# Seven places instead of four for split weight pieces in the first of two fused transformer blocks

## Chip, cores and metric

The program runs on one NeuronCore of a Trainium2 chip. The metric is the device time of one execution in microseconds (us). Before the change three runs gave 1586.46, 1587.95 and 1588.61 us; their median, 1587.95 us, is the time before. The core holds five engines that work side by side: PE (matmul), DVE and POOL (element-wise), ACT (activation, copies) and SP, which here only starts transfers from HBM.

## What is computed

Two blocks follow one another on 256 tokens of width 1024, all in fp32. The first has two layers; each is a mix of three attentions and then an MLP with a hidden width of 4096. The second block is a mixer (latent attention and an mLSTM) and a mixture of 16 experts, of which each takes 32 tokens.

```python
def hybrid_layer(x, mem, pos, g_mix, w_in, w_pa, w_pb, w_pm, w_o, g_mem, w_mkv, g_mlp, w_up, w_down):
    h = rms_norm(x, g_mix)
    z = h @ w_in
    ...
    x = x + y @ w_o
    hm = rms_norm(x, g_mlp)
    x = x + jnp.square(jax.nn.relu(hm @ w_up)) @ w_down
    return x
```

The second block adds `mixer(...)` and `ec_moe(...)`: each expert computes `silu(xs @ w_gate) * (xs @ w_up) @ w_down` on the tokens that it takes, scaled by its gate.

## The kernel before

**A weight's way to PE.** `load_w` (L311) loads a tile of weights of 1 MB, `wr`, in one transfer on SP's queue; there are four such buffers (`WR`). `pieces` (L328) cuts the tile into four pieces of 128 x 512 and splits each into two parts, since PE takes a rounded fp32 format here: ACT casts the piece into its high part (L346), and DVE (L352), or POOL for a set share of the pieces (L350), subtracts that from the piece for the low part. Both go into a *place* of the tile `wh`, which holds `WH` = 4 of them, used in turn. PE multiplies a piece in 12 matmuls (`three` L355, which calls `mm` L289: high by high, high by low, low by high). A place comes free when PE has read its piece, and a `wr` buffer when its four pieces have been split. So a split can run at most four pieces ahead of PE.

**The activations' way to PE.** The residual is `xT`, in eight parts. At each hand-over from one half of a layer to the next, `split_and_sum` (L482) adds the last product to `xT` (L478, DVE), splits each part into `hx` (ACT L426, DVE L427), and squares it (ACT L489) and sums the squares on POOL (L491). `rstd_cols` makes 1/rms of the sum (matmul `ps_mlp`, DVE L462, POOL L463), `bcast_rows` spreads it (matmul `ps_bc`, DVE L472).

**The MLP.** `mlp` (L864) runs over 16 columns of 256 hidden units. `up(c)` is 48 matmuls of four pieces, and piece j needs parts 2j and 2j+1 of `hx`. `relu2` (L881, L882, L424) turns `up` into `ux`; `accumulate` multiplies it by `w_down`, 48 matmuls `dn` for each column, two columns behind (`LAG` = 2). PE's program after a hand-over is up(0), `ps_mlp`, 12 matmuls of up(1), `ps_bc`, the rest of up(1), up(2), and the first `dn`.

**Side work in the MLPs.** `mod_rows` (L924) multiplies rows of `w_modT` on DVE and sums them (the result is `macc`). In the second MLP `context` also squares and sums `ctxT` (`ssc`: ACT L447 and L450, POOL L451), scales it (`modt` L968, DVE) and splits it (`xh`: ACT L974, DVE L975), and `gate_weights` (L1083 to L1097) prepares small weights on DVE. A row of `mod_rows` is tied behind the split before it by `tc.issue_after(behind[0])`.

**Order.** PE's order is that of the program. The orders of DVE, ACT, POOL and SP come from a scheduler at build time: it places work by priority, and splits carry a raised one (`tc.high_priority(offset=HP)`). Where a place is not yet free in the scheduler's reckoning, the split comes later in the order. In the first layer's MLP the list `HMQ` = (None, None, 0, 2) ties piece 2 of up(0) behind part 0 of `hx`, and piece 3 behind part 2; the second layer's MLP has no such tie. Two pools matter: `whl` holds `wh` for the whole program, and `b1p` lies on the right side of the on-chip memory until `b1.close()` (L1582), after the second layer's MLP; behind that, expert weights (`ew`, from `load_e`, transfers at L1502) use its room.

Of the kernel before, what the change touches and what calls it, by code (L numbers as in the profile page):

```python
# [9 lines left out]
FR = mybir.dt.float32r  # L10
# [6 lines left out]
PIECE = 512  # L17
WR = 4
WH = 4
LAG = 2  # L20
TL = 20
FH = 4.0
# [212 lines left out]
def drain(gen):  # L235
    for _ in gen:
        pass
# [3 lines left out]
def fused_kernel(ctx: ExitStack, tc: tile.TileContext, I, out):  # L241
# [30 lines left out]
    b1p = b1.enter_context(tc.tile_pool(name="b1p", bufs=1, side="right"))  # L272
# [8 lines left out]
    def vc(n, j=0, w=1):  # L281
        o = vcols[n][0] + j
        return vbuf[:, o:o + w]
# [27 lines left out]
    def load_w(src, parts=1):  # L311
        K, n = src.shape[1], src.shape[2]
        t = wrp.tile([128, 2048], FT, tag="wr", name="wr")
        v = t[:, :K * n].rearrange("p (k n) -> p k n", k=K)
        for a in range(0, K, K // parts):
            nc.sync.dma_start(out=v[:, a:a + K // parts], in_=src[:, a:a + K // parts])
        return v

    share = [0.0, 0.0]
    whx = whl.tile([128, 2, WH * PIECE], FR, tag="w", name="wh")  # L320
    whi, wlo = whx[:, 0], whx[:, 1]
    np_ = [0]

    hold = []

# [2 lines left out]
    def pieces(v, small=0):  # L328

        K, n = v.shape[1], v.shape[2]  # L330
        step = max(1, PIECE // n)
        for k0 in [*range(small), *range(small, K, step)]:
            k1 = k0 + 1 if k0 < small else min(K, k0 + step)
            for n0 in range(0, n, PIECE):
                n1 = min(n, n0 + PIECE)
                src = v[:, k0:k1, n0:n1]
                p0 = np_[0] % WH * PIECE
                np_[0] += 1
                sz = (k1 - k0) * (n1 - n0)
                hv = whi[:, p0:p0 + sz].rearrange("p (k n) -> p k n", k=k1 - k0)  # L340
                lv = wlo[:, p0:p0 + sz].rearrange("p (k n) -> p k n", k=k1 - k0)
                with ExitStack() as es:
                    es.enter_context(tc.high_priority(offset=HP))
                    for ins in hold.pop(0) if hold else ():
                        es.enter_context(tc.issue_after(ins))
                    A.copy(hv, src)  # L346
                    share[1] += share[0]
                    if share[1] >= 1:
                        share[1] -= 1
                        behind[1] = G.tensor_tensor(lv, src, hv.bitcast(FT), op=OP.subtract).ins  # L350
                    else:
                        behind[0] = V.tensor_tensor(lv, src, hv.bitcast(FT), op=OP.subtract).ins  # L352
                yield k0, k1, n0, hv, lv
# [6 lines left out]
    def hi_lo(pl, K, tag, **kw):  # L360

        t = pl.tile([128, 2, K, 256], FR, tag=tag, name=tag, **kw)
        return t[:, 0], t[:, 1], t
# [37 lines left out]
    def accumulate(w, dn, x2, kx, first, last):  # L401

        def one(k, m, hv, lv, m0, kk):
            ms = slice((m - m0) * 128, (m - m0 + 1) * 128)
            three(dn[m // 2][:, (m % 2) * 256:(m % 2) * 256 + 256], hv[:, kk, ms], lv[:, kk, ms], x2[:, :, kx + k],
                  first and k == 0 and m % 2 == 0, last and k == 1)

        if last:

            for q in range(4):  # L410
                for k0, k1, _, hv, lv in pieces(w[:, :, q * 256:(q + 1) * 256]):
                    for m in (2 * q, 2 * q + 1):
                        for k in range(k0, k1):
                            one(k, m, hv, lv, 2 * q, k - k0)
        else:
            for k0, k1, n0, hv, lv in pieces(w):
                for k in range(k0, k1):
                    for m in range(n0 // 128, n0 // 128 + hv.shape[2] // 128):
                        one(k, m, hv, lv, n0 // 128, k - k0)
# [24 lines left out]
    def square_sum(xv, K, ssum, tp):  # L444
        for k in range(K):
            if k == 0:
                A.square(ssum, xv[:, 0])  # L447
            else:
                t = tp.tile([128, 256], FT, tag="sq", name="sq", bufs=2)
                A.square(t, xv[:, k])  # L450
                G.tensor_tensor(ssum, ssum, t, op=OP.add)  # L451

    def rstd_cols(ssum, n, nm, bank=None):

        ps = (bank or acc_tile)("ps_" + nm)
        halves = [ssum] if len(ssum.shape) == 2 else [ssum[:, i] for i in range(ssum.shape[1])]
        for t in range(2):
            for i, v in enumerate(halves):
                mm(ps[:, t:t + 1], v[:, t * 128:(t + 1) * 128], ones[:, 0:1], t + i == 0, i == len(halves) - 1)
        r = sm.tile([128, 2], FT, tag="rc_" + nm, name="rc_" + nm, bufs=2)  # L460
        with tc.high_priority(offset=HR):
            V.tensor_scalar(r, ps[:, 0:2], 1.0 / n, EPS, op0=OP.mult, op1=OP.add)  # L462
            G.tensor_tensor(r, r, mhalf[:, 0:2], op=OP.pow)  # L463
        return r
# [17 lines left out]
    def split_and_sum(dn, g0, tp, queue=()):  # L482
        hh, hl, hx = hi_lo(tp, 8, "hx")
        ssum = tp.tile([128, 256], FT, tag="ssum", name="ssum", bufs=2)
        parts = []
        for k in updated(dn):
            parts.append(split_x(xT[:, k], hh[:, k], hl[:, k], vc(g0[0], g0[1] + k)))
            sq = ssum if k == 0 else tp.tile([128, 256], FT, tag="sq", name="sq", bufs=2)
            A.square(sq, xT[:, k])  # L489
            if k:  # L490
                G.tensor_tensor(ssum, ssum, sq, op=OP.add)  # L491
        hold[:] = [() if k is None else parts[k] for k in queue]
        return (hh, hl, hx), ssum
# [370 lines left out]
    def mlp(l, mp, side, dn):  # L864

        urs = [mp.tile([128, 2, 256], FT, name=f"ur{i}") for i in range(2)]
        us = [hi_lo(mp, 2, f"ux{i}") for i in range(LAG + 1)]
        xs, ssum = split_and_sum(dn, ("g_mlp", l * 8), mp, () if l else HMQ)
# [8 lines left out]
        def relu2(o):  # L877
            r = urs[nu[0] % 2]
            uh, ul, ux = us[nu[0] % (LAG + 1)]
            nu[0] += 1  # L880
            V.scalar_tensor_tensor(r, pair(o), 0.0, both(rb), op0=OP.max, op1=OP.mult)  # L881
            A.square(r, r)  # L882
            split_x(r, uh, ul)
            return ux
# [6 lines left out]
        for c in range(1, 16):  # L891
# [7 lines left out]
            cur.append(relu2(o2))  # L899
            if c >= LAG:  # L900
                accumulate(load_w(I["w_down"][l, c - LAG]), dn, cur.pop(0), 0, c == LAG, False)
            for _ in range(side[1] + (l == 0 and c in MS1)):
                next(side[0], None)
        for c in range(16 - LAG, 16):
            accumulate(load_w(I["w_down"][l, c]), dn, cur.pop(0), 0, False, c == 15)
# [640 lines left out]
    with tc.tile_pool(name="mp1", bufs=1, reuse_waits="tile") as mp:  # L1546
        src = mp.tile([128, 8, 256], FT, name="ctxT")
        nc.sync.dma_start(out=src, in_=I["ctxT"])

        def context():  # L1550
            yield
            ssum = mp.tile([128, 256], FT, tag="rbc", name="ssc")
            square_sum(src, 8, ssum, mp)
            yield
            yield
            rcc = rstd_cols(ssum, 1024, "in", fl_tile)
            yield
            rbc = mp.tile([128, 256], FT, tag="rbc", name="rbc")
            bcast_rows(rcc, rbc, fl_tile)
            yield from modulated(src, rbc, sc1[:, 1], modT[:, 1, 0:8], mp, into(ch, cl))  # L1560

        def chain(*gens):
            for g in gens:
                yield from g

        def side():
            rg = mod_rows(8, 24, (0,), mp)
            cg = context()
            bg = chain(diagonals("wv4", 0), gate_weights(wg, mp), diagonals("wq4", 1))
            for n in range(40):  # L1570
                if n % 2 == 0:
                    next(cg, None)
                next(rg, None)
                next(bg, None)
                yield

        sg = side()
        dn = mlp(1, mp, (sg, 2), dn)
        drain(sg)
        V.tensor_tensor(modT[:, 0, 16:48], macc[:, 0, 16:48], vc("b_mod", 16, 32), op=OP.add)  # L1580
        V.scalar_tensor_tensor(sc1[:, 2], modT[:, 0, 32:40], 1.0, vc("n2", 0, 8), op0=OP.add, op1=OP.mult)
    b1.close()  # L1582
    xs = hh, hl, _ = hi_lo(x2p, 8, "hx")
    mlx = ctx.enter_context(ExitStack())
# [176 lines left out]
    for j in range(4):  # L1761
# [5 lines left out]
        for i in range(2):  # L1767
            k = 2 * j + i
# [205 lines left out]
    for ci, n in enumerate(LAST):  # L1974
        c0, w = i * 128, n * 128
        for _ in range(n):
            cc = (i % 4) * 128
            for kh in range(2):
                parts = expert_tile()
                kp = 4 // len(parts)  # L1980
                for k in range(4):
                    t = parts[k // kp].rearrange("p (k e c) -> p k e c", e=4, c=128)
# [45 lines left out]
```

## Time and profile before

| | |
|---|---|
| median of 3 runs | 1587.95 us (1586.46 to 1588.61) |
| the profiled execution's own time | 1588.72 us |
| its span in the trace | 1586.9 us |
| mean granted clock of PE over the span | 0.948 of full speed |
| PE, DVE, ACT, POOL busy | 1387.1, 898.2, 675.9, 232.7 us |
| first block | 0 to about 803.6 us of the span |
| experts | from about 1156 us to the end |

The span is what the trace covers; the execution's own time lies 1.8 us above it. Rows of a timeline give start, length, engine, line, operation, output <- inputs, and in brackets how long the engine was idle just before and which work ended that wait. A name such as `wh` stands for all places of that name.

### The profile page before, as it was taken

The numbers are of one execution on the slowest core, as the hardware profiler recorded it, in microseconds if no ns is written. First come the engines' busy times: TensorE is split into PE (matmuls) and PEld (weight loads), VectorE is DVE, ScalarE is ACT, GpSimd is POOL, SyncE is SP. The second block draws the span as 40 slices with busy tenths as digits, with TensorE's granted clock in tenths as the row PEclk, the third lists the DMA queues.
The fourth block names the chain that finished last, engine by engine and source line by source line (L and its number), as shares of the span: only waits on it lengthen the run. The fifth ranks groups of instructions, "written<-read, shape, count | busy, mean of one in ns | idle before, by whom it ended". The sixth has DMA issues, their size and how long they took to land. (4 is left out here: it accounts for less than half of the span.)

```text
span 1586.9 us, 27036 instructions
## 1 busy us (share of the span) xinstructions
PE 1387.1 (87%) x10903; PEld 1153.8 (73%) x10903; DVE 898.2 (57%) x1615; ACT 675.9 (43%) x1341; POOL 232.7 (15%) x204
## 2 busy tenths in 40 slices
PE   8999999999999999999988999999888665656565
PEld 7999999999999998999987889989743111111113
DVE  8876688777787578897789775885320000000001
ACT  7566555555557556555556666555310000000001
POOL 3100022121210015322144200210100000000000
PEclk9999999999999999999998999999989878787978
DMA  8544446666543456767763322374979999999997
GB/s 315 178 145 143 160 168 248 244 222 229 196 145 132 166 185 230 266 252 279 268 250 108 134 78 80 131 275 145 366 302 424 427 428 427 428 428 426 428 427 322
DMA packets 50557, 404.87 MB, mean 255 GB/s; under 512 B 5504, under 2 KB 7424, under 8 KB 14464
## 3 DMA queue, kind: packets, MB, share of 16 engines
q1 hardware_dynamic: 50288, 403.04, 65.6%
q8 instruction: 85, 1.39, 0.3%
q14 instruction: 40, 0.33, 0.1%
q10 hardware_dynamic: 144, 0.11, 0.0%
HBM read 402.08 MB, written 1.05 MB: 254 GB/s over the span
## 5 line engine op out<-in xcount | busy, mean ns | idle before, releaser
L346 ACT CAST wh<-wr 128x512 fp32r<-128x512 f32 (+1 forms) x647 | 394.1, 616 | 351.5 <-PE up L289 81.2
L352 DVE TENSOR_TENSOR wh<-wr,wh 128x512 fp32r<-128x512 f32 (+1 forms) x563 | 403.8, 727 | 154.7 <-ACT wh L346 152.5
L289 PE MATMUL up<-hx,wh 128*128 128x256 f32 x1536 | 194.5, 285 | 7.6 <-DVE wh L352 4.9
L289 PEld LDWEIGHTS up<-hx,wh 128*128 128x128 f32 x1536 | 187.7, 192 | 10.9 <-DVE wh L352 6.6
L289 PE MATMUL dn<-ux,wh 128*128 128x256 f32 x1536 | 189.7, 283 | 0.4 <-DVE wh L352 0.4
L289 PEld LDWEIGHTS dn<-ux,wh 128*128 128x128 f32 x1536 | 186.6, 192 | 1.0 <-DVE wh L352 0.8
L350 POOL TENSOR_TENSOR wh<-wr,wh 128x512 fp32r<-128x512 f32 (+1 forms) x84 | 117.6, 1400 | 463.5 <-ACT wh L346 434.1
L1946 DVE TENSOR_TENSOR ew<-up,ew 128x512 f32<-128x512 f32 x8 | 5.5, 692 | 251.4 <-PE up L289 251.4
L289 PE MATMUL gate<-hx,wh 128*128 128x256 f32 x1152 | 141.6, 284 | 0.0
L289 PEld LDWEIGHTS gate<-hx,wh 128*128 128x128 f32 x1152 | 139.1, 192 | 1.4 <-issue 1.4
L289 PE MATMUL y<-ew 128*32 128x128 f32 (+1 forms) x896 | 76.0, 488 | 42.5 <-DMA ew<-in_w_e_down_dram 41.8
L289 PE MATMUL up<-ew,xsr 128*32 128x512 f32 x384 | 65.4, 815 | 52.7 <-DMA ew<-in_w_e_up_dram 52.7
L289 PE MATMUL gate<-ew,xsr 128*32 128x512 f32 x384 | 60.9, 764 | 50.2 <-DMA ew<-in_w_e_gate_dram 50.2
L1940 ACT ACTIVATE ew<-gate 128x512 f32<-128x512 f32 x8 | 4.8, 597 | 208.6 <-PE gate L289 207.3
L289 PEld LDWEIGHTS y<-ew 128*32 128x32 f32 x896 | 28.1, 122 | 88.2 <-DMA ew<-in_w_e_down_dram 50.7
L289 PEld LDWEIGHTS up<-ew,xsr 128*32 128x32 f32 x384 | 12.4, 131 | 106.6 <-DMA ew<-in_w_e_up_dram 74.7
L289 PEld LDWEIGHTS gate<-ew,xsr 128*32 128x32 f32 x384 | 11.9, 124 | 96.5 <-DMA ew<-in_w_e_gate_dram 64.3
L289 PE MATMUL z<-hx,wh 128*128 128x256 f32 x576 | 74.1, 286 | 4.0 <-ACT wh L346 1.2
L289 PE MATMUL tanh<-hx,wh 128*128 128x256 f32 x576 | 77.0, 287 | 0.2 <-DVE wh L352 0.2
L289 PEld LDWEIGHTS z<-hx,wh 128*128 128x128 f32 x576 | 70.4, 191 | 6.8 <-DVE hx L427 1.6
L289 PEld LDWEIGHTS tanh<-hx,wh 128*128 128x128 f32 x576 | 71.5, 191 | 1.2 <-DVE wh L352 0.5
L924 DVE SCALAR_TENSOR_TENSOR wr<-wr,srow 128x1024 f32<-128x1024 f32 x48 | 68.5, 1432 | 0.0
(451 smaller groups left out, 1991.8 us busy)
## 6 DMA issues: line engine op xcount, KB each, us to landing
ew<-in_w_e_up_dram SPq DMA_DIRECT2D x26, 2048.0 KB, 22.1
ew<-in_w_e_down_dram SPq DMA_DIRECT2D x25, 2048.0 KB, 21.4
ew<-in_w_e_gate_dram SPq DMA_DIRECT2D x24, 2048.0 KB, 21.4
wr<-in_w_up_dram SPq DMA_DIRECT2D x32, 1024.0 KB, 4.9
wr<-in_w_down_dram SPq DMA_DIRECT2D x32, 1024.0 KB, 5.4
wr<-in_w_gates_dram SPq DMA_DIRECT2D x24, 1024.0 KB, 4.8
wr<-in_w_modT_dram SPq DMA_DIRECT2D x24, 1024.0 KB, 4.9
wr<-in_w_in_dram SPq DMA_DIRECT2D x24, 1024.0 KB, 4.8
```

The costliest lines, as they stand in the source:

```text
L289: PE.matmul(o, l, r, start=st, stop=sp, skip_group_check=True)
L346: A.copy(hv, src)
L350: behind[1] = G.tensor_tensor(lv, src, hv.bitcast(FT), op=OP.subtract).ins
L352: behind[0] = V.tensor_tensor(lv, src, hv.bitcast(FT), op=OP.subtract).ins
L924: V.scalar_tensor_tensor(d, w[:, j], 0.5, srow[v], op0=OP.mult, op1=OP.mult, accum_out=macc[:, v, 2 * i + j:2 * i + j + 1])
L1940: A.activation(h[:, j * 512:(j + 1) * 512], gate[j], AF.Silu)
L1946: V.tensor_tensor(h[:, c], up[j], h[:, c], op=OP.mult)
```

## The change

Three more places are allocated in the pool `b1p`, as a second tile `wx_` that is also named `wh`. A list `places` holds the seven in turn: each new piece takes the one that was used longest ago. At the end of the first block the three are struck from the list, and four are used from there on. Nothing is said of `HMQ`, of priorities or of the share of POOL.

```diff
@@ -17,6 +17,7 @@
 PIECE = 512
 WR = 4
 WH = 4
+WX = 3
 LAG = 2
 TL = 20
 FH = 4.0
@@ -318,8 +319,10 @@
 
     share = [0.0, 0.0]
     whx = whl.tile([128, 2, WH * PIECE], FR, tag="w", name="wh")
-    whi, wlo = whx[:, 0], whx[:, 1]
-    np_ = [0]
+    wx_ = b1p.tile([128, 2, WX * PIECE], FR, name="wh")
+
+    places = [(t[:, 0, a:a + PIECE], t[:, 1, a:a + PIECE], t is whx) for t, n in ((whx, WH), (wx_, WX))
+              for a in range(0, n * PIECE, PIECE)]
 
     hold = []
 
@@ -334,11 +337,9 @@
             for n0 in range(0, n, PIECE):
                 n1 = min(n, n0 + PIECE)
                 src = v[:, k0:k1, n0:n1]
-                p0 = np_[0] % WH * PIECE
-                np_[0] += 1
+                places.append(places.pop(0))
                 sz = (k1 - k0) * (n1 - n0)
-                hv = whi[:, p0:p0 + sz].rearrange("p (k n) -> p k n", k=k1 - k0)
-                lv = wlo[:, p0:p0 + sz].rearrange("p (k n) -> p k n", k=k1 - k0)
+                hv, lv = [p[:, :sz].rearrange("p (k n) -> p k n", k=k1 - k0) for p in places[-1][:2]]
                 with ExitStack() as es:
                     es.enter_context(tc.high_priority(offset=HP))
                     for ins in hold.pop(0) if hold else ():
@@ -1579,6 +1580,7 @@
         drain(sg)
         V.tensor_tensor(modT[:, 0, 16:48], macc[:, 0, 16:48], vc("b_mod", 16, 32), op=OP.add)
         V.scalar_tensor_tensor(sc1[:, 2], modT[:, 0, 32:40], 1.0, vc("n2", 0, 8), op0=OP.add, op1=OP.mult)
+    places[:] = [p for p in places if p[2]]
     b1.close()
     xs = hh, hl, _ = hi_lo(x2p, 8, "hx")
     mlx = ctx.enter_context(ExitStack())
```

PE's order does not change at all. On DVE, ACT, POOL and SP nearly all moved instructions are splits: throughout the first block, each other instruction now has three more casts ahead of it than before. SP issues two small side loads (`ctxT`, `wgt`) one place later. Behind `b1.close()` all orders agree.

In the rows below a number behind a name tells buffers apart: `wh_95` are the old places (in both versions), `wh_96` the new ones, and `wr_` names the loaded tile, whose number the change shifts by one. Line numbers of the new version lie one higher.

DVE at the hand-over to the first layer's MLP, before. `wr_2689` is up(0), `wr_2754` is up(1), `dn0` and `dn1` are the last product of the attention half:

```order
L478 TENSOR_TENSOR xT_84<-xT_84,dn0_2169 128x512 x2
L352 TENSOR_TENSOR wh_95<-wr_2689,wh_95 128x512
L478 TENSOR_TENSOR xT_84<-xT_84,dn1_2170 128x512
L427 SCALAR_TENSOR_TENSOR hx_2641<-xT_84,vbuf_83,hx_2641 128x256
L478 TENSOR_TENSOR xT_84<-xT_84,dn1_2170 128x512
L427 SCALAR_TENSOR_TENSOR hx_2641<-xT_84,vbuf_83,hx_2641 128x256 x4
L352 TENSOR_TENSOR wh_95<-wr_2689,wh_95 128x512
L427 SCALAR_TENSOR_TENSOR hx_2641<-xT_84,vbuf_83,hx_2641 128x256 x3
L352 TENSOR_TENSOR wh_95<-wr_2689,wh_95 128x512
L352 TENSOR_TENSOR wh_95<-wr_2754,wh_95 128x512 x2
L462 TENSOR_SCALAR rc_mlp_2750<-ps_mlp_2747 128x2
```

The same place with the change (`wr_2690` is up(0), `wr_2755` up(1)):

```order
L479 TENSOR_TENSOR xT_84<-xT_84,dn0_2170 128x512 x2
L353 TENSOR_TENSOR wh_96<-wr_2755,wh_96 128x512 x2
L479 TENSOR_TENSOR xT_84<-xT_84,dn1_2171 128x512 x2
L428 SCALAR_TENSOR_TENSOR hx_2642<-xT_84,vbuf_83,hx_2642 128x256 x2
L353 TENSOR_TENSOR wh_96<-wr_2755,wh_96 128x512
L428 SCALAR_TENSOR_TENSOR hx_2642<-xT_84,vbuf_83,hx_2642 128x256 x3
L353 TENSOR_TENSOR wh_95<-wr_2690,wh_95 128x512
L428 SCALAR_TENSOR_TENSOR hx_2642<-xT_84,vbuf_83,hx_2642 128x256 x3
L353 TENSOR_TENSOR wh_95<-wr_2690,wh_95 128x512
L353 TENSOR_TENSOR wh_95<-wr_2755,wh_95 128x512
L925 SCALAR_TENSOR_TENSOR modd_2832,macc_497<-wr_2830,srow_496 128x1024
L463 TENSOR_SCALAR rc_mlp_2751<-ps_mlp_2748 128x2
```

Three pieces of up(1) now stand ahead of up(0)'s pieces 2 and 3, which are still tied behind `hx`; the first `hx` stands behind both additions to `xT`; and a row of `mod_rows` stands ahead of `rc_mlp`.

ACT at the hand-over to the second layer's MLP, before. `wr_6966`, `wr_7031` and `wr_7108` are up(0), up(1) and up(2):

```order
L426 ACTIVATE hx_6918<-xT_84,vbuf_83 128x256
L346 CAST wh_95<-wr_6966 128x512
L489 ACTIVATE sq_6959<-xT_84 128x256
L346 CAST wh_95<-wr_7031 128x512 x3
L447 ACTIVATE ssc_7228<-ctxT_6911 128x256
L346 CAST wh_95<-wr_7031 128x512
L450 ACTIVATE sq_7230<-ctxT_6911 128x256
L450 ACTIVATE sq_7233<-ctxT_6911 128x256
L450 ACTIVATE sq_7236<-ctxT_6911 128x256
L346 CAST wh_95<-wr_7108 128x512
```

The same place with the change (up(0) to up(2) are `wr_6967`, `wr_7032`, `wr_7109`; `wr_7171` is the first tile of `w_down`):

```order
L490 ACTIVATE sq_6960<-xT_84 128x256
L347 CAST wh_96<-wr_7032 128x512 x2
L347 CAST wh_95<-wr_7109 128x512 x3
L448 ACTIVATE ssc_7229<-ctxT_6912 128x256
L451 ACTIVATE sq_7231<-ctxT_6912 128x256
L347 CAST wh_95<-wr_7109 128x512
L451 ACTIVATE sq_7234<-ctxT_6912 128x256
L451 ACTIVATE sq_7237<-ctxT_6912 128x256
L451 ACTIVATE sq_7240<-ctxT_6912 128x256
L347 CAST wh_96<-wr_7171 128x512
```

Three casts of up(2) now stand ahead of the first square of `ctxT`, where before only up(1) had been cast; all of up(2) is cast ahead of the third square of `ctxT`.

DVE in the middle of the second MLP, before (`wr_7657` and `wr_7719` are an up and a down tile):

```order
L352 TENSOR_TENSOR wh_95<-wr_7657,wh_95 128x512
L472 COPY rbc_7638<-ps_bc_7639 128x256
L968 SCALAR_TENSOR_TENSOR modt_7643<-ctxT_6911,sc1_86,rbc_7638 128x256
L968 SCALAR_TENSOR_TENSOR modt_7777<-ctxT_6911,sc1_86,rbc_7638 128x256
L975 SCALAR_TENSOR_TENSOR xh_6907<-modt_7643,modT_85,xh_6907 128x256
L968 SCALAR_TENSOR_TENSOR modt_7908<-ctxT_6911,sc1_86,rbc_7638 128x256
L352 TENSOR_TENSOR wh_95<-wr_7719,wh_95 128x512
L975 SCALAR_TENSOR_TENSOR xh_6907<-modt_7777,modT_85,xh_6907 128x256
L975 SCALAR_TENSOR_TENSOR xh_6907<-modt_7908,modT_85,xh_6907 128x256
L352 TENSOR_TENSOR wh_95<-wr_7719,wh_95 128x512
```

The same place with the change (`wr_7658`, `wr_7720`):

```order
L353 TENSOR_TENSOR wh_96<-wr_7658,wh_96 128x512
L425 TENSOR_TENSOR ux2_6918<-ur1_6915,ux2_6918 128x512
L353 TENSOR_TENSOR wh_95<-wr_7720,wh_95 128x512 x2
L473 COPY rbc_7639<-ps_bc_7640 128x256
L353 TENSOR_TENSOR wh_95<-wr_7720,wh_95 128x512
L969 SCALAR_TENSOR_TENSOR modt_7644<-ctxT_6912,sc1_86,rbc_7639 128x256
L969 SCALAR_TENSOR_TENSOR modt_7778<-ctxT_6912,sc1_86,rbc_7639 128x256
L353 TENSOR_TENSOR wh_96<-wr_7720,wh_96 128x512
L976 SCALAR_TENSOR_TENSOR xh_6908<-modt_7644,modT_85,xh_6908 128x256
L976 SCALAR_TENSOR_TENSOR xh_6908<-modt_7778,modT_85,xh_6908 128x256
```

Where `modt` began behind the last piece of `wr_7657`, it now begins behind three pieces of the tile after it.

## Rows read from the trace of the kernel before

**Rows 1.** Busy time of each engine over the span, instructions

```profile
PE 1387.1 (87%) x10903; PEld 1153.8 (73%) x10903; DVE 898.2 (57%) x1615; ACT 675.9 (43%) x1341; POOL 232.7 (15%) x204
```

**Rows 2.** Stretches, from:to, length, busy (instructions), granted clock, DMA share, GB/s

```profile
226.26:248.55 22.29, 19.86 (x153) 18.38 (x152) 20.84 (x32) 14.38 (x29) 9.49 (x10) 1.00 0.44 159
415.75:425.46 9.71, 7.54 (x53) 6.61 (x53) 9.68 (x13) 8.49 (x21) 5.80 (x7) 1.00 0.30 109
608.76:631.97 23.21, 19.90 (x152) 18.44 (x151) 18.72 (x29) 15.97 (x36) 15.88 (x17) 1.00 0.49 175
632.00:672.70 40.70, 40.70 (x342) 40.70 (x341) 33.03 (x46) 21.66 (x37) 16.12 (x15) 1.00 0.75 276
672.73:705.67 32.94, 30.72 (x244) 29.48 (x243) 32.09 (x53) 16.90 (x32) 7.59 (x5) 1.00 0.59 206
250.00:415.00 165.00, 165.00 (x1378) 165.00 (x1377) 121.13 (x187) 87.02 (x143) 31.74 (x22) 1.00 0.65 236
1210.00:1587.00 377.00, 223.44 (x1732) 62.92 (x1730) 17.95 (x33) 10.62 (x28) 0.70 (x1) 0.82 0.98 416
```

**Rows 3.** PE's waits up to 803.6: line, awaited work, us, times, longest

```profile
PE up L289 <- DVE wh L352: 4.9, 7, 1.1
PE up L289 <- DVE hx L427: 1.3, 1, 1.3
...
PE up L289 <- POOL wh L350: 1.1, 2, 0.6
...
PE dn L289 <- DVE wh L352: 0.4, 2, 0.2
```

**Rows 4.** The chain that ended last, its last and longest piece

```profile
1154.54 426.19 issue
```

**Rows 5.** SP queue's waits, 780 to 1210: expert loads behind PE

```profile
SPq L1502 <- PE gate L289: 23.3, 6, 15.9
```

**Rows 6.** Timeline of DVE in the hand-over to the second MLP

```profile
612.77 2.71 DVE L427 SCALAR_TENSOR_TENSOR hx<-xT,vbuf,hx 128x256 fp32r<-128x256 f32 x3
```

**Rows 7.** Timeline of PE in the same hand-over

```profile
616.13 1.46 PE L289 MATMUL up<-hx,wh 128*128 128x256 f32 x10 [1.09 <-DVE wh L352]
...
627.73 4.41 PE L289 MATMUL up<-hx,wh 128*128 128x256 f32 x34 [0.72 <-DVE wh L352]
631.97 5.92 PE L289 MATMUL dn<-ux,wh 128*128 128x256 f32 x48
```

**Rows 8.** Timeline of ACT in the same hand-over

```profile
625.53 0.42 ACT L450 ACTIVATE sq<-ctxT 128x256 f32<-128x256 f32 x1 [1.51 <-POOL ssc L451]
```

**Rows 9.** Timeline of POOL in the same hand-over

```profile
608.41 6.78 POOL L491 TENSOR_TENSOR ssum<-ssum,sq 128x256 f32<-128x256 f32 x7 [8.30 <-ACT sq L489]
...
619.27 4.29 POOL L451 TENSOR_TENSOR ssc<-ssc,sq 128x256 f32<-128x256 f32 x3
```

**Rows 10.** Groups of DVE from 672.73 to 705.67: busy, mean ns

```profile
L352 DVE TENSOR_TENSOR wh<-wr,wh 128x512 fp32r<-128x512 f32 x18 | 14.2, 804 | 0.0
L924 DVE SCALAR_TENSOR_TENSOR wr<-wr,srow 128x1024 f32<-128x1024 f32 x5 | 7.1, 1431 | 0.0
```

**Rows 11.** Costliest groups of the page: the split on DVE

```profile
L352 DVE TENSOR_TENSOR wh<-wr,wh 128x512 fp32r<-128x512 f32 (+1 forms) x563 | 403.8, 727 | 154.7 <-ACT wh L346 152.5
```

**Rows 12.** Timeline of DVE in the hand-over to the first MLP

```profile
226.46 0.69 DVE L478 TENSOR_TENSOR xT<-xT,dn 128x512 f32<-128x512 f32 x1 [0.99 <-PE dn L289]
...
231.36 1.23 DVE L352 TENSOR_TENSOR wh<-wr,wh 128x512 fp32r<-128x512 f32 x1
```

**Rows 13.** Timeline of PE in the same hand-over

```profile
235.73 0.50 PE L289 MATMUL ps_mlp<-cbuf,ssum 128*128 128x1 f32 x4
...
244.38 4.33 PE L289 MATMUL up<-hx,wh 128*128 128x256 f32 x34 [0.31 <-DVE wh L352]
```

**Rows 14.** Timeline of DVE in the hand-over to the second layer's attention

```profile
419.00 5.34 DVE L427 SCALAR_TENSOR_TENSOR hx<-xT,vbuf,hx 128x256 fp32r<-128x256 f32 x6
```

**Rows 15.** Timeline of the SP queue around the end of the first block

```profile
804.02 1.02 SPq L1502 DMA_DIRECT2D ew<-in_w_e_gate_dram  x2
```

## The prediction

> **What bounds the kernel now.** I read the busy times first. PE works 1387.1 of 1586.9 us and DVE 898.2 [rows 1], so PE is the engine to follow, but that share is a mean over stages. Stretches come next [rows 2]: from 250 to 415 us PE is busy for all 165.00 us, with 1378 matmuls, 0.1197 us each, at a granted clock of 1.00. No number of places helps there, since PE waits for nothing. The stretches around the hand-overs differ. I name four by their length in [rows 2]: **B** (22.29 us, into the first MLP), **C** (9.71 us, into the second layer's attention), **D** (23.21 us, into the second MLP) and **E** (32.94 us, in the middle of the second MLP). B and D hold 144 full matmuls and 6 small ones, 150 x 0.1197 = 18.0 us of work, so 4.3 and 5.2 us are lost. C holds 48 and 2, 6.0 us of work, so 3.7 are lost. E holds 240 and 2, 29.0 us, so 4.0 are lost.
>
> PE's waits in the first block say on what [rows 3]: `up` waits 4.9 us in 7 pieces for DVE's low part of a weight, 1.1 us for POOL's, `dn` 0.4 us for DVE's, and `up` 1.3 us for the activations' `hx`. Those for `wh` are what more places can shorten; a wait for `hx` is not.
>
> The last question is whether time won before 803.6 us arrives at the end. The chain that ended last is one piece without a releaser from 1154.54 us on, 426.19 us long [rows 4], and from 1210 us the 16 DMA engines are busy for 0.98 at 416 GB/s [rows 2]: the experts are bound by their loads. But the loads before that are let go by PE: between 780 and 1210 us SP's queue waits 23.3 us on `gate` matmuls before expert loads [rows 5]. So an earlier first block moves PE's releases, the loads and the end by the same amount. I carry gains over one to one.
>
> **The change part by part.** It adds no work: the same casts, subtractions and matmuls, in PE's same order. What it gives is a lead of three more pieces, and 3 x 12 x 0.1197 = 4.3 us of PE's work. In the full stretches this is worth nothing, as PE is already full. It also lets each `wr` buffer go up to 4.3 us sooner, and asks for each load as much sooner; DMA is busy 0.65 of the time between 250 and 415 us, 0.75 between D and E and 0.59 in E [rows 2], so I cost that at nothing. What is then left is hand-over by hand-over.
>
> *D.* up(0) needs the last parts of `hx`. DVE ends those at 612.77 + 2.71 = 615.48 [rows 6], and the last six matmuls or so need 0.72 after that: 616.2. PE in fact ended up(0) at 616.13 + 10 x 0.12 = 617.33, after waiting 1.09 us for a split [rows 7] that stood behind `hx`. With the change all of up(0) is split ahead of `xT`, as the order of ACT and DVE there shows, so 1.1 us go. Behind it, ACT's casts of up(2) stood behind squares of `ctxT`, which wait on POOL's additions, 1.51 us in one case [rows 8]; PE lost another 0.72 us right before 627.73 [rows 7]. Three of those casts now stand ahead of the squares. So PE would run from 616.2 through 96 matmuls and 6 small ones, 102 x 0.1197 = 12.2 us, to 628.4, against 631.97 [rows 7]: **3.6 us** won. What is late next is `ux` for the first `dn`: ACT can begin it behind the fifth square, which waits for POOL's third addition, at 619.27 + 4.29 = 623.56 [rows 9], or 622.5 if the 1.1 us move it too. Four short instructions of at most 0.8 us each follow, 625.7, so it stays covered. The bounds are 1.1 us (up(0) alone) and 5.2 us (all that is lost).
>
> *E.* DVE is busy 32.09 of 32.94 us here [rows 2]. Its 18 splits take 804 ns each, against 727 ns as the mean of the kernel, and the rows of `mod_rows` 1431 ns [rows 10, 11]: DVE falls behind PE by 4.0 us in all. The lead of 4.3 us is a little more than this. If it is there when E begins, PE waits for nothing. The order has three pieces more ahead of the first `modt`. The bounds are 32.94 - 32.09 = 0.85 us (no lead left when E begins, DVE's pace sets the end) and 4.0 us. I take **3.3 us**, nearer the upper end since 4.3 exceeds 4.0, with something off for a ring that may not be quite full.
>
> *B.* Here up(0)'s pieces 2 and 3 are tied behind `hx`, so the places go to up(1). The chain from 226.46 us to PE's end of up(0) at 235.73 [rows 12, 13] gets one more split, while POOL adds squares. A split there took 1.23 us [rows 12], against 0.73 as the mean of the kernel [rows 11]; I take 1.0 us of loss. In exchange later splits are early, so the wait of 0.31 us at 244.38 [rows 13] goes, and some of what DVE does behind it is easier; I give back 0.5 us. That makes **0.5 us slower**, with 2.7 us slower as the far end (1.23, and 1.43 for the `mod_rows` row that now stands ahead of `rc_mlp`) and 1 us faster as the near one. The slack that hides `mod_rows` is the 48 matmuls of up(1), 5.7 us, which don't need `rc_mlp`.
>
> A rule of the Trainium skill speaks against this edit. The page "SBUF — State Buffer", section "Who interferes with whom", says that a DVE instruction with two inputs in SBUF contends with a GpSimd instruction that reads SBUF, and that the shared pair of ports is an exclusive lock, not a split of bandwidth. POOL's additions last 6.78 / 7 = 0.97 us each [rows 9]; by that rule a split that comes second would take as much as 0.73 + 0.97 = 1.70 us, B would lose another 0.5 us, and the sum below would be 5.9 instead of 6.4. The row of 1.23 us agrees that the two slow one another, by less than a whole addition, and I go by the row.
>
> *C.* PE waits for `hx` alone: six instructions, from 419.00 for 5.34 us, to 424.34 [rows 14], and with 0.72 us behind them the stretch is as good as over. The order of DVE stays as it is. Nothing.
>
> *The end of the block.* The first expert loads go out at 804.02 us [rows 15], after PE's last `dn` (about 803.6), and lie in the room that held the new places. PE's last read of them is no later than that end, so this adds no wait. Behind `b1.close()` four places are used as before. Nothing.
>
> **Sum.** 3.6 + 3.3 - 0.5 = 6.4 us less. The profiled execution took 1588.72 us, 0.77 above the median, so it would take 1582.3, and a median of runs 1587.95 - 6.4, about **1581.5 us**. What a measurement of this kernel can tell from no change is 0.2%, 3.2 us.
>
> **The rivals.**
>
> *1. DVE or `hx` is the bound, and the lead is spent before it is needed.* For it: C loses 3.7 us to `hx` alone, and in E DVE is 97% busy. Against it: in E the waits are for `wh`, and DVE has 40.70 - 33.03 = 7.7 us free between D and E [rows 2], where three more splits need 3 x 0.80 = 2.4. Then D gives 1.1, E 0.85 and B takes 0.5: 1.5 us less, **1586.5 us**. It decides if the ring is less than one piece fuller when E begins. Chance 0.14.
>
> *2. Early splits stand in the way of `hx`.* A split of a later tile, ready by ACT, is taken by DVE ahead of an `hx` on which PE waits now. At B the order does this. If each costs what the row beside POOL shows, B loses 1.23 + 1.43, and one such split more at D another 1.23 us, 3.9 us in all; if E's ring is empty as well, nothing pays for it: **1591.9 us**, slower. Against it: at D the order shows as many splits among the `hx` as before. It decides if `up`'s wait for `hx` (1.3 us now) grows past 4 us. Chance 0.08.
>
> *3. Full cover.* Nothing but `hx` stalls PE: D gives 5.2, E 4.0, and B gains as much as it loses: 9.2 us less, **1578.8 us**. Against it: the last `hx` in D sets 616.2. Chance 0.10.
>
> *4. The change doesn't do what it says:* the splits are let go by something else, the `wr` loads say, and run no further ahead. DMA in E at 0.59 speaks against that. 1588 us, chance 0.02.
>
> My forecast has the rest, 0.66. Forecast and rival 3 are faster by over 0.2%: 0.76. Rivals 1 and 4 lie within: 0.16. Rival 2 is slower: 0.08. The range goes from 1577.5 us (rival 3, with 1 us gained at B) to 1587.0 us, which takes in rival 1 and the forecast's lower bounds (D 1.1, E 0.85, B -0.5 to -1). It leaves out rivals 2 and 4, and the ends of the others, some 0.15 in all.
>
> **What would show it.** Right: D's first `dn` at 19.6 us after the start of its up(0), instead of 23.2; E's waits for `wh` gone, its 240 matmuls in 29 to 30 us; `up`'s and `dn`'s waits for `wh` in the first block below 2 us in all, from 6.4; C unchanged; B within 1 us of 22.29; the rest of the kernel as long as before from the end of the block on. Wrong: `up` waiting longer for `hx` at B and D (rival 2); E still 32 us or more with DVE full (rival 1); or the block shorter and the experts' end where it was, so that the loads don't follow PE.

## The result and the profile after

The changed kernel took 1570.4 us, the median of 4 runs (1568.68 to 1572.26), against 1587.2 us for the kernel before on the same chip (4 runs); the ratio is 0.9894 with a 95% interval from 0.9877 to 0.9911. That is 16.8 us, or 1.1%, less: faster, as was forecast, but by more than twice the 6.4 us forecast, and outside the range. The profiled execution took 1572.26 us, 16.5 less than the one before.

The two lines of the page of the changed kernel that answer to [rows 1], and the last piece of its chain of waits, which answers to [rows 4]:

```profile
span 1570.5 us, 27054 instructions
...
PE 1372.3 (87%) x10903; PEld 1138.6 (72%) x10903; DVE 914.0 (58%) x1615; ACT 666.6 (42%) x1341; POOL 242.3 (15%) x204
```

```profile
1138.58 425.70 issue
```

PE is 87% busy as before, but in 14.8 us less, with the same 10903 matmuls. The end is the same piece of 426 us, 16 us sooner: the loads of the experts did follow PE.

Stretches of the changed kernel, with the columns of [rows 2]: D, E, two stretches of 36 and of 48 matmuls in one run of `gate` matmuls, and the experts.

```profile
602.50:623.75 21.25, 18.88 (x152) 18.05 (x151) 20.77 (x28) 16.07 (x37) 19.37 (x19) 1.00 0.56 214
664.05:692.78 28.73, 28.73 (x244) 28.46 (x243) 28.51 (x45) 14.20 (x28) 7.93 (x5) 1.00 0.58 210
520.94:525.03 4.09, 4.09 (x39) 4.09 (x38) 2.60 (x5) 2.19 (x4) 0.00 (x0) 1.00 0.72 244
525.03:530.79 5.76, 5.76 (x51) 5.76 (x50) 3.44 (x6) 3.14 (x6) 0.00 (x0) 1.00 0.52 189
1195.00:1570.00 375.00, 224.13 (x1724) 61.84 (x1716) 17.25 (x33) 10.47 (x27) 0.69 (x1) 0.81 0.99 417
```

D takes 21.25 us where it took 23.21, and E 28.73 where it took 32.94. So far this is what the prediction spoke of. The third and fourth row are not. Both are without any wait, at a granted clock of 1.00. The first covers three pieces, 36 matmuls, in 4.09 us, 113.5 ns each (a stretch also counts the two or three that overlap its edge); the second covers four pieces, 48 matmuls, in 5.76 us, 120.0 ns each. This pattern of 36 and 48 repeats through the run: three places of seven are the new ones. In the first MLP the matmuls of the new places took 117.8 ns instead, so that it won only 1.2 us (table below).

Timeline of PE in the kernel before, in the last third of the second MLP, and then in E of the changed kernel (48 matmuls a row):

```profile
774.79 5.92 PE L289 MATMUL dn<-ux,wh 128*128 128x256 f32 x48
780.55 5.92 PE L289 MATMUL up<-hx,wh 128*128 128x256 f32 x48
```

```profile
675.48 5.76 PE L290 MATMUL up<-hx,wh 128*128 128x256 f32 x48
681.08 5.76 PE L290 MATMUL dn<-ux,wh 128*128 128x256 f32 x48
686.68 6.27 PE L290 MATMUL up<-hx,wh 128*128 128x256 f32 x48
```

Before, one row of 48 starts 5.76 us after the other, 120.0 ns a matmul. With the change it is 5.60, 116.7 ns. PE waited for nothing between the two rows in either. The prediction had called such stretches full and left them there.

PE's waits up to 800 us in the changed kernel, for [rows 3]:

```profile
PE up L290 <- DVE hx L428: 2.2, 3, 1.0
PE ps_bc L294 <- POOL rc_mlp L464: 1.8, 2, 1.3
PE up L290 <- DVE wh L353: 1.6, 3, 0.8
...
PE up L290 <- ACT hx L427: 1.0, 1, 1.0
...
PE dn L290 <- POOL wh L351: 0.3, 1, 0.3
```

The waits of `up` and `dn` for low parts in `wh` fell from 6.4 to 1.9 us. New is the wait of `ps_bc` for `rc_mlp`, 1.8 us, and `up`'s wait for `hx` grew from 1.3 to 3.2 us, of which 1.0 is for ACT's part.

Stage by stage, from the starts of the same matmuls in the two traces (B from the last `dn` of the attention half to the first `dn` of the MLP; F from the first matmul of the second block to `ps_fin`; "lead alone" is an experiment below):

| stage | before | changed | lead alone | forecast of the lead |
|---|---|---|---|---|
| B | 22.41 | 24.23 | 24.29 | +0.5 |
| first MLP, B to C | 166.92 | 165.70 | 166.92 | 0 |
| C | 9.63 | 9.62 | 9.63 | 0 |
| second attention, C to D | 183.66 | 180.17 | 183.46 | 0 |
| D | 23.21 | 21.25 | 21.17 | -3.6 |
| E | 32.94 | 28.73 | 29.00 | -3.3 |
| second block begins at | 803.59 | 789.41 | 799.64 | -6.4 |
| F | 16.44 | 14.69 | 14.71 | 0 |

Of the 14.2 us won by 803.59, 10.2 are not the lead's. The prediction's own stretch B starts later, with the first `up`; measured so, it took 22.95 us in the changed kernel and 23.01 with the lead alone, against 22.29. The rest of B's loss lies ahead of that start.

### The profile page after: what moved, and what is told of

It reads as the page before. It is cut to its first block, busy times and chain, and to the rows that moved or that the text cites. A ratio compares the mean times of both kernels' runs of the same rounds, so it can differ in the third digit from the quotient of the medians.

```text
span 1570.5 us, 27054 instructions
## 1 busy us (share of the span) xinstructions
PE 1372.3 (87%) x10903; PEld 1138.6 (72%) x10903; DVE 914.0 (58%) x1615; ACT 666.6 (42%) x1341; POOL 242.3 (15%) x204
## 3 DMA queue, kind: packets, MB, share of 16 engines
HBM read 402.08 MB, written 1.05 MB: 257 GB/s over the span
## 5 line engine op out<-in xcount | busy, mean ns | idle before, releaser
L347 ACT CAST wh<-wr 128x512 fp32r<-128x512 f32 (+1 forms) x647 | 388.3, 615 | 295.5 <-PE up L290 55.7
L353 DVE TENSOR_TENSOR wh<-wr,wh 128x512 fp32r<-128x512 f32 (+1 forms) x563 | 418.4, 756 | 128.6 <-ACT wh L347 124.7
L290 PE MATMUL up<-hx,wh 128*128 128x256 f32 x1536 | 190.9, 282 | 4.9 <-DVE hx L428 2.2
L351 POOL TENSOR_TENSOR wh<-wr,wh 128x512 fp32r<-128x512 f32 (+1 forms) x84 | 122.3, 1457 | 438.0 <-ACT wh L347 369.5
```

The lines of the kernel that those rows point to most:

```text
L290: PE.matmul(o, l, r, start=st, stop=sp, skip_group_check=True)
```

## The experiments

The theory after the trace was that two things had happened. The lead gave what it gives at D and E; and matmuls whose weights lie in the new tile follow one another faster, because of where that tile lies. The program's memory plan says where: the old tile begins at byte 50336 of a partition, the new one at 192096, and `hx` of the attention at 66720. Old tile and `hx` are a multiple of 128 bytes apart, and so are `ux`, `zq` and the other `hx`; the new tile is 64 bytes off. The rivals: the lead itself makes the pace; the right part of the memory does; or the weights' own offset does.

**Seven places, the new tile moved by 64 bytes.**

```diff
-    wx_ = b1p.tile([128, 2, WX * PIECE], FR, name="wh")
+    wxt = b1p.tile([128, 2 * WX * PIECE + 16], FR, name="wh")
+    wx_ = wxt[:, :2 * WX * PIECE].rearrange("p (i n) -> p i n", i=2)
```

> The change as it is (seven places), but the tile of the three new places begins 64 bytes lower in SBUF, so that it lies at the same offset from a multiple of 128 bytes (32) as the four old places and hx do; in the change it lies at 96. Nothing else moves. In the profile of the change matmuls on weights from the new places follow one another after 113.3 ns, on those from the old after 120 ns. Theory A (the offset of the weights against that of the other operand sets PE's pace): every matmul at 120 ns, the 11 us of pace are lost, and what the lead alone gives is left: about 5 us less than before, 1582 us. Theory B (the pace comes from the lead itself, since PE no longer waits for a split): new places still at 113 ns, 1570 us. Theory C (the part of SBUF counts, far right against left, whatever the offset): as B, 1570 us.

Measured: 1579.3 us, ratio 0.9954 (0.9939 to 0.9969), 7.8 us less than before instead of 16.8. In the run of `gate` matmuls the pace of the new places went from 113.3 to 118.7 ns, start to start. So it is not the lead, and not the part of the memory. It is not quite the 120 of the old places either; this tile lies 128 bytes off modulo 256, which the next but one takes up.

**Four places, moved against the rest.** Unused bytes behind the old tile move all that lies above it (`hx`, `ux`, `zq`); ahead of it, the tile as well.

```diff
+    ctx.enter_context(tc.tile_pool(name="pada", bufs=1)).tile([128, 16], FT, name="pada")
     whl = ctx.enter_context(tc.tile_pool(name="whl", bufs=1, reuse_waits="tile"))
+    ctx.enter_context(tc.tile_pool(name="padb", bufs=1)).tile([128, 16], FT, name="padb")
```

64 bytes behind:

> The kernel before (four places), with 64 unused bytes behind the tile of the places: the weights stay at offset 32 of 128, hx, ux and all that lies above go to 96. No lead is added. Theory A (relative offset): all matmuls of the first block at about 113 ns, some 118 in the first MLP, 25 to 35 us less than before, about 1555 to 1562 us, and more if the second block gains as well. Theory B (lead): nothing, 1587 us. Theory C (part of SBUF): nothing, 1587 us. Theory D (the absolute offset of the weights alone, 96 being the good one): nothing, 1587 us.

64 bytes ahead:

> The kernel before, with 64 unused bytes ahead of the tile of the places: weights, hx and ux all go from offset 32 to 96 of 128. Theory A (relative offset): 120 ns throughout, 1587 us. Theory B and C: 1587 us. Theory D (absolute offset of the weights): 113 ns throughout the first block, 1555 to 1562 us.

64 bytes ahead and 64 behind:

> The kernel before, with 64 unused bytes ahead of the tile of the places and 64 behind: the weights go to offset 96 of 128, all the rest stays at 32. Theory A and theory D: 113 ns, 1555 to 1562 us. Theory B and C: nothing, 1587 us.

32 bytes behind:

> The kernel before (four places at offset 32), with 32 unused bytes behind them: hx, ux and the rest lie at offset 64, 32 bytes from the weights modulo 128. If only equal offsets collide: 113 to 118 ns a matmul, as at 64 bytes. In the kernel before, 108 matmuls on qx (offset 64) against weights at 32 followed one another after 117 ns, and those on kvx at 64 after 117.5 on the average; if that carries over, 117 ns, about 1574 us.

96 bytes behind:

> The kernel before (four places at offset 32), with 96 unused bytes behind them: hx, ux and the rest lie at a multiple of 128, 96 bytes above the weights. If only equal offsets slow PE: 113 to 118 ns. If it goes by the distance, 32 bytes up being as good as 32 down: 117 ns as there (1568 us). With 64 bytes behind the places, kvx and qx came to lie at a multiple of 128 and their matmuls took 119 to 120 ns; if that carries over, 119 to 120 ns, and 1583 to 1587 us.

The same stretch, 530 to 580 us, inside the run of `gate` matmuls, in the kernel before, with 64 bytes ahead (all moves together), 64 behind, 64 on both sides, 32 behind and 96 behind. In all of them PE is busy for the whole 50.00 us at a clock of 1.00; what differs is how many matmuls it does in it.

```profile
530.00:580.00 50.00, 50.00 (x419) 50.00 (x418) 33.09 (x49) 26.47 (x43) 2.91 (x2) 1.00 0.49 169
```

```profile
530.00:580.00 50.00, 50.00 (x419) 50.00 (x418) 32.69 (x50) 26.91 (x44) 2.73 (x2) 1.00 0.48 169
```

```profile
530.00:580.00 50.00, 50.00 (x427) 50.00 (x426) 36.77 (x55) 26.38 (x43) 4.53 (x3) 1.00 0.51 184
```

```profile
530.00:580.00 50.00, 50.00 (x444) 50.00 (x443) 38.76 (x58) 27.10 (x45) 4.53 (x3) 1.00 0.55 193
```

```profile
530.00:580.00 50.00, 50.00 (x431) 50.00 (x430) 37.72 (x57) 27.16 (x45) 4.53 (x3) 1.00 0.51 178
```

```profile
530.00:580.00 50.00, 50.00 (x419) 50.00 (x419) 32.70 (x49) 26.82 (x44) 2.78 (x2) 1.00 0.48 169
```

| weights and the other operand | distance modulo 128 | matmuls in 50 us | ns, start to start | time |
|---|---|---|---|---|
| before | 0 | 419 | 120.0 | 1587.2 |
| 64 ahead, both move | 0 | 419 | 120.0 | 1587.04, ratio 1.0 (0.999 to 1.0009) |
| 64 behind | 64 | 427 | 113.3 or 117.8 | 1573.41, ratio 0.9912 (0.9891 to 0.9932) |
| 64 ahead and behind | 64 | 444 | 113.3 or 117.8 | 1568.41, ratio 0.9877 (0.986 to 0.9894) |
| 32 behind | 32 | 431 | 116.8 | 1568.41, one run |
| 96 behind | 96 | 419 | 120.0 | 1584.55, one run |

The distance decides, not the weights' own offset (64 ahead changes it, and nothing happens). With four places and no lead, 64 bytes give 14 and 19 us; the second is more than the change itself (16.8). The expectation of 25 to 35 us was too high for two reasons that the traces show: in long runs the pace settled at 113.3 or at 117.8 ns, and the splits began to hold PE back (with 64 bytes on both sides D took 23.33 us, no less than the 23.21 before, though each of its matmuls was shorter). The pace changed often where PE had been interrupted, but not only there; why it takes the one or the other was not found. The run with 96 bytes begins its second block at 803.15 us, as before (803.59); what it is shorter comes after that, and is told below.

**The lead alone.** The new tile 192 bytes lower, a multiple of 256 from `hx`, as the old one is.

```diff
+    wxt = b1p.tile([128, 2 * WX * PIECE + 48], FR, name="wh")
```

> Seven places, the new ones 192 bytes lower than in the change, so that their distance to hx is a multiple of 256 bytes, as that of the old ones is. With 64 bytes (offset 32 of 128, but 128 of 256 away from hx) the matmuls on them still took 118.7 ns instead of 120, some 3 us over the first block. If equal places modulo 256 are what makes 120 ns, all take 120 ns now and what is left is the lead alone: the forecast's 6.4 us, 1580 to 1582 us. If the 118.7 had another cause, 1578 to 1580 us as there.

The stretch from 530 to 580 us:

```profile
530.00:580.00 50.00, 50.00 (x419) 50.00 (x418) 32.52 (x50) 27.42 (x44) 1.79 (x2) 1.00 0.50 175
```

Measured: 1580.62 us against 1587.31, ratio 0.9961 (0.9946 to 0.9976), 6.2 us by the ratio, and 419 matmuls in the stretch, as before. All matmuls take 120 ns. So the 118.7 of the first run came from the 128 bytes, and the pace goes by the distance modulo 256 rather than 128. This is the kernel that the prediction described, and its time is the prediction's 1581.5 within one us; how much of that is luck is told below. The column "lead alone" above is from its trace.

**One more place instead of three**, with the unused bytes of the first run (the new tile a multiple of 128 from `hx`).

```diff
-WX = 3
+WX = 1
```

> Five places, all at offset 32: a lead of one more piece, 1.44 us of PE's work, instead of three. Theory of the lead as in the forecast: in the middle of the second MLP, where DVE falls behind by 4.0 us, one piece gives about 1.4 us of the 4.0 that three pieces gave; the whole about 1584 us. If any fifth place is enough (the stall is a wait of one split on the place just ahead), all of it comes back: 1579 to 1580 us.

Measured: 1577.91 us, ratio 0.9934 (0.9919 to 0.9949). The whole does not tell the theories apart, so I take the stages. E took 30.51 us, 2.4 less than before; three places gave 3.9 to 4.1. So the gain at E grows with the lead, though the first piece was worth more than its 1.44 us. B lost 1.3 us instead of 1.9, and D won 1.75 instead of 2.0. B, D and E together gave 2.9 us, three places 4.1. The second block began at 799.36 us, as with the lead of three alone (799.64), but here the matmuls of the new place, 128 bytes off, are quicker too: the first MLP took 166.30 us instead of 166.92, so this start is not the lead's alone. What made the whole shorter lies in the second block, where this kernel's orders also differ a little from those of the kernel before. So three places gave more than one in these stages, but were not shown to give more all in all: the intervals overlap.

How far the second block varies by itself is shown by the run with 96 bytes, whose orders are those of the kernel before. From 825 to 925 us, before and in that run (the granted clock is the third number from the end):

```profile
825.00:925.00 100.00, 88.96 (x655) 78.70 (x654) 80.35 (x158) 58.49 (x119) 27.18 (x23) 0.93 0.34 122
```

```profile
825.00:925.00 100.00, 88.76 (x677) 79.51 (x675) 80.81 (x161) 61.10 (x124) 27.25 (x24) 0.97 0.34 120
```

At 0.97 instead of 0.93 it does 22 more matmuls in 100 us, and that is where its 2.7 us come from. The kernel with one more place had 0.95 there, the lead alone 0.93. So of differences of up to 3 us between kernels a part can be this.

**ps_bc later.** In both MLPs behind 24 matmuls of up(1) instead of 12, with the tile of the first run.

```diff
                 next(g)
                 next(g)
+                next(g)
+                next(g)
                 bcast_rows(rc, rb, fl_tile)
```

> Seven places at offset 32 (lead alone, 1579.3 us), and in both MLPs the broadcast ps_bc stands behind 24 matmuls of up(1) instead of 12. In the change PE waits at ps_bc for rc_mlp, 1.33 us in the second MLP and 0.45 in the first, and 1.8 in all with seven places at offset 32, which it did not before. If this wait is what kept the hand-over into the second MLP from giving the 3.6 us of the forecast, it goes: ps_bc below 0.3 us of waiting, that hand-over about 1.3 us shorter, and in all 1 to 1.8 us less than 1579.3. If PE then waits as long for ux or a split instead, no change.

PE in D:

```profile
618.42 0.43 PE L294 MATMUL ps_bc<-cbuf,rc_mlp 128*128 128x128 f32 x2
...
622.58 5.99 PE L290 MATMUL up<-hx,wh 128*128 128x256 f32 x48 [0.89 <-DVE ur L883]
```

Measured: 1578.03 us, ratio 0.9938 (0.9924 to 0.9953). The wait at `ps_bc` is gone, and 0.89 us of waiting for `ur` stand behind the 24 matmuls that follow it: up(2) needs the accumulator that `relu2` frees, and `relu2` needs what `ps_bc` brings. D became only 0.4 us shorter (20.85), and the whole 1.3 us, too little to be told from no change. B did gain: 23.58 after 24.24. The second expectation, a wait in place of the wait, held for D.

**POOL's share later.** In D of the changed kernel DVE and POOL stood so:

```profile
609.28 2.37 DVE L353 TENSOR_TENSOR wh<-wr,wh 128x512 fp32r<-128x512 f32 x2
611.58 0.15 DVE L463 TENSOR_SCALAR rc_mlp<-ps_mlp 128x2 f32<-128x2 f32 x1
```

```profile
609.39 1.71 POOL L351 TENSOR_TENSOR wh<-wr,wh 128x512 fp32r<-128x512 f32 x1 [0.32 <-ACT wh L347]
611.80 1.62 POOL L464 TENSOR_TENSOR rc_mlp<-rc_mlp,mhalf 128x2 f32<-128x2 f32 x1 [0.69 <-DVE rc_mlp L463]
```

Two splits on DVE lasted 2.37 us while POOL made one of its own (1.71), so `rc_mlp` came at 611.58; POOL's power (it makes 1/rms of it) then took 1.62 us beside a row of `mod_rows`, and PE, which needs it for `ps_bc`, waited 1.33:

```profile
607.65 2.62 PE L290 MATMUL up<-hx,wh 128*128 128x256 f32 x17 [1.03 <-DVE hx L428]
...
613.48 0.43 PE L294 MATMUL ps_bc<-cbuf,rc_mlp 128*128 128x128 f32 x2 [1.33 <-POOL rc_mlp L464]
...
623.75 2.52 PE L290 MATMUL dn<-ux,wh 128*128 128x256 f32 x20
```

The first of these rows shows up(0) ended by `hx`, as forecast. The experiment, on the lead alone, keeps POOL's split away from there:

```diff
-        share[:] = SHM[l], 0.0
+        share[:] = SHM[l], -0.8 * l
```

> As the run before this one (seven places, lead alone), and in the second MLP POOL takes its first share of a split four pieces later, so that no split stands on POOL between the squares and rc_mlp. In the change two splits on DVE took 2.37 us there beside POOL's, rc_mlp came behind them at 611.58, and PE waited 1.33 us at ps_bc. If this is what kept the hand-over into the second MLP at 2.0 of the 3.6 us: the two splits take 1.3 us, ps_bc waits 0.5 us or less, the hand-over is 0.8 us or more shorter. If the row of mod_rows beside POOL's power is what counts: ps_bc still waits about 1 us.

The two splits on DVE, and PE in D:

```profile
616.52 1.28 DVE L354 TENSOR_TENSOR wh<-wr,wh 128x512 fp32r<-128x512 f32 x2
```

```profile
619.28 0.43 PE L294 MATMUL ps_bc<-cbuf,rc_mlp 128*128 128x128 f32 x2
...
629.62 2.56 PE L290 MATMUL dn<-ux,wh 128*128 128x256 f32 x20
```

Measured in one run: 1577.14 us. The splits took 1.28 us, `ps_bc` did not wait, and D took 19.72 us, 3.5 less than before. With POOL's split moved, the row of `mod_rows` moved behind as well, so the two parts of the delay were not separated; together they account for nearly all that D fell short of the forecast, in one run.

**All places 64 bytes off, with the lead.** The change, with 64 bytes on both sides of the old tile.

> The change (seven places) with 64 unused bytes ahead of the old tile of places and 64 behind it: all seven now lie at offset 96 of 128 and the other operands at 32. If lead and pace are two separate gains that add up, this gives both: the lead's 8 us (seven places at offset 32 ran 1579.3 against 1587.1) and the pace of four places at offset 96 (1568.4, 19 us), more where the splits no longer hold PE back: 1558 to 1562 us. If the faster PE only runs into the splits, no better than four places at 96, 1567 us.

Measured: 1552.7 us, ratio 0.9772 (0.9755 to 0.9789), 35 us less than before and better than the 1558 expected. Lead and pace do more together than apart: the second block begins 13.5 us sooner than with four places and 64 bytes on both sides, where the lead alone brought 4.0. The difference does not lie at the hand-overs or in E (29.67 us here, 32.28 there: 2.6 less, where the lead alone gave 3.9), but in full stretches, 5.7 us of it in the first MLP: 158.15 us here, 163.83 there. PE waits for no weight in either stretch; the pace stood at 113.3 ns here and at 117.8 there. Whether the lead brings the better level about is not shown; the run of `gate` matmuls is at 113.3 ns in both (443 and 444 in the 50 us).

**The best of these.** The same, with the later `ps_bc` and without the tie of up(0)'s pieces.

```diff
-HMQ = (None, None, 0, 2)
+HMQ = ()
```

> Seven places, all at offset 96 of 128 against 32 (1552.7 us), ps_bc behind 24 matmuls instead of 12, and no tie of up(0)'s pieces 2 and 3 to hx in the first MLP. The forecast's loss at the hand-over into the first MLP came from splits of up(1) that go ahead while those two are tied. If so, up(0) no longer waits for wh there (0.76 and 0.61 us in the change), and the hand-over is about 1.5 us shorter with the later ps_bc: 1550 to 1552 us. If hx then takes the place of that wait, 1552 to 1553 us.

PE in B, where up(0) now runs from its second piece through without waiting for a split:

```profile
222.93 5.23 PE L292 MATMUL up<-hx,wh 128*128 128x256 f32 x35 [0.85 <-DVE hx L430]
```

Measured: 1549.4 us, ratio 0.9763 (0.9747 to 0.9779). B took 21.45 us, 2.6 less than the 24.04 with the tie and the earlier `ps_bc`, of which the run with the later `ps_bc` showed 0.7 to be `ps_bc`'s. This is the fastest kernel of the study, 21 us under the change.

## Why the prediction was wrong

**The step that failed** is the one on the full stretches: "PE is busy for all 165.00 us ... No number of places helps there, since PE waits for nothing", and "in the full stretches this is worth nothing, as PE is already full". The number of places did not help there; their address did. PE was busy at 120 ns a matmul, and 113.3 or 117.8 was to be had. No rival named this, and with it 10.2 of the 14.2 us that the first block won were missed. The rows did not show that 120 was not PE's best; [rows 2] gave 0.1197 us in its full stretches because there the other operands lie a multiple of 256 bytes from the one tile of weights. But the trace of the kernel before did show it, in the second block, where `uq` multiplies `qx`, which lies 32 bytes further on than a multiple of 256:

```profile
1033.17 4.36 PE L289 MATMUL uq<-qx,wh 128*128 128x256 f32 x36
1037.37 0.40 PE L289 MATMUL v<-wh,kvx 128*128 128x512 f32 x1
```

36 matmuls of the same shape in 4.20 us are 116.7 ns each. The question could have been raised from this row, and from the change itself, which adds a second tile at another address and not only more of the first.

**The lead, taken by itself, came out in the sum, in part by luck.** Forecast 6.4 us, measured 6.2 by the ratio (3.8 to 8.6 by its interval). But the three terms that make up the 6.4 gave 4.0 by the start of the second block, and 1.7 came from a stage that was put at nothing. Part by part:

- *E* was right: between 640 and 720 us the waits for `wh` fell to 0.5 us in the changed kernel and to none with the lead alone, and the lead alone gained 3.9 us (forecast 3.3, upper bound 4.0).
- *D* was half right. up(0) ended behind `hx`, 1.05 us sooner in the changed kernel, as forecast (1.1). But "what is late next" was not `ux`: it was `rc_mlp`, on which PE's order has `ps_bc` wait after 12 matmuls. D gave 2.0 instead of 3.6 us; with POOL's split out of the way it gave 3.5.
- *B* was right in sign, and mis-sized: 1.9 us slower instead of 0.5, inside the bounds. The forecast counted one more split on DVE. It left out that the first `up` now waits for ACT's part of `hx`, 1.00 us where it did not wait before:

```profile
226.26 0.28 PE L289 MATMUL up<-hx,wh 128*128 128x256 f32 x1
```

```profile
224.06 0.38 PE L290 MATMUL up<-hx,wh 128*128 128x256 f32 x1 [1.00 <-ACT hx L427]
```

On ACT casts of later pieces now stand ahead of that `hx`, and the last of them began at 222.98, after waiting 0.69 us for PE to free its place. Without the tie this wait is still there (1.00 us in the last experiment). Behind it `up` waits for `hx` and for `wh` in turn, and the 0.5 us that I gave back did not come, since `ps_bc` waits there too. The splits beside POOL's additions took 1.22 to 1.24 us, as [rows 12] had shown. They did not take the 1.70 us that was estimated as the most by the rule of the Trainium skill, page "SBUF — State Buffer", section "Who interferes with whom". The rule's direction holds in D, where two splits beside POOL's took 2.37 us, against 1.28 without it.
- *C* was right: 9.63 and 9.62 us.
- *The end of the block* was called nothing and gave 1.7 us: the waits of `kvl` and `xm` for a split, just behind `b1.close()`, went from 1.3 us to almost none. That the pieces of the second block then find their old places free sooner is likely, and was not tried.
- *That gains carry to the end* held: the chain's last piece begins 15.96 us sooner.

**The rivals.** The second, splits in the way of `hx`, is what B shows, on ACT; its point of 4 us of waiting was not reached (3.2). Full cover came closest in time, 1578.8, for another reason. D's and E's gains were not swallowed, as the first had it.

## What to carry to other kernels

A busy PE without waits is not a PE at its best: compare the start-to-start time of equal matmuls whose operands lie at different addresses before calling a stretch full. When a change adds a buffer, the new address is part of the change; try the old buffers at the new offset, and the new one at the old offset, before giving the gain to the extra depth. A deeper ring helps where the engine that fills it falls behind for a while, up to that deficit, and it puts more filling work ahead of whatever shares that engine at a hand-over.

## What the runs showed of the hardware that was not expected

- A matmul of 256 fp32r columns (the rounded format) on 128 x 128 weights followed its predecessor after 120.0 ns when weights and the other operand lay a multiple of 256 bytes apart, after 118.7 at 128, after 116.8 with the other operand 32 bytes up, after 113.3 or 117.8 at 64, and after 120.0 on the average at 96, all at a granted clock of 1.00. The `uq` matmuls agree, since `qx` lies 32 bytes further on: 36 of them took 4.20 us before (32 apart), 4.32 with 64 bytes behind (96 apart) and 4.27 with 96 behind (128 apart). What in the chip makes the distance count, no run shows.
- It counts also where the weights are the moving operand: in the change, the `v` matmuls took 115 ns on the new places and 119 on the old. Not by the same amounts, though: with 32 and 96 bytes behind they took 118.3 and 118.1 ns, the others 116.8 and 120.0.
- At 64 bytes the pace stood at one of two levels, 113.3 or 117.8 ns, often for a whole stage.
- 64 unused bytes on both sides of a tile were worth 19 us of 1587, with the order of every engine unchanged.
